# Attention scores of two maps in one tile of three PSUM banks, and a third bank for transposes and value products

## The chip, the cores and the metric

The kernel runs on one core of a Trainium2 chip. The metric is device time in microseconds (us) of one execution, as the median of several. TensorE (PE) multiplies matrices; its weight loads are shown as an engine of their own (PEld). VectorE (DVE) and ScalarE (ACT) read its results out of PSUM, which has eight banks of 512 float32 values for each of 128 partitions. Each engine takes its instructions in the order of its queue.

## What is computed

One inference step of a network of two layers, on 512 latent tokens and 128 prompt tokens, handled as one tile of 640 columns. The change lies in the first (even) layer, whose mixer has two kinds of attention heads. Four heads of kind A are differential: two attention maps on the same values, the second subtracted with a weight. Four pairs of heads of kind B are grouped-query attention, two heads of a pair on two halves of the partitions. In both, a block of 128 queries has two maps of scores, each softmaxed by itself:

```python
# kind A: two maps on the same values
a1 = block_attend(qa[:, :, None, :, :DH_A], k_a[..., :DH_A], v_a)[:, :, 0]
a2 = block_attend(qa[:, :, None, :, DH_A:], k_a[..., DH_A:], v_a)[:, :, 0]
oa = rms_norm(a1 - lam * a2, P['a_subln_g'][i]) * (1.0 - lam_init)
# kind B
ob = block_attend(qg, k_b, v_b)
# block_attend, for a block of 128 queries
sc = jnp.einsum('bgrqd,bgtd->bgrqt', qi, k).astype(F32) * scale
p = jax.nn.softmax(sc, axis=-1).astype(v.dtype)
return jnp.einsum('bgrqt,bgte->bgrqe', p, v)
```

Latent queries (blocks 0 to 3) see 256 cached and 512 own keys, 768 in all; prompt queries (block 4) see their own 128. A head so has four wide blocks and one narrow one, and the eight heads (counting a pair as one) 32 and 8.

## The kernel before

`even` (from L660) does the even layer. After the first projections it opens its PSUM pools: "g" has two banks for the whole kernel, and here "m" gets two banks and "S" two tiles of two banks (L683). The eight heads run in the order a0, a1, b0, b1, a2, b2, a3, b3 (`EV_HEADS`, L45). Beside them runs a stream of other work, `filling` (L906): the projections of the heads to come (tile "g"), the modulation of later layers (weights `wa`), norms and scalings of finished heads, and the first five eighths of the output projection. `in_turn` deals out head and filling by the numbers of `EV_FILL` (L47). On top of that the framework orders each engine's queue by a timeline of its own, so the queue isn't the order of the code.

A block of a head goes like this. `scores` (L753) takes two tiles of "S", one for each map, and multiplies: each map in two halves of 384 keys, one to a bank, and each half in two matmuls, since queries and keys are split into a rounded part and a rest (index `e`). Then for each map DVE takes the negated maximum `nm` (L766) and ACT the exponential with its sum, into `pr` (L768; four buffers). `scores` of block i+1 is called before block i goes on. For kind A (`attn_a`, L786) DVE joins the two maps into one (L798). `turned` (L773) transposes the probabilities on PE, three tiles of 128 to a bank of "m", and DVE or ACT copies them out to `PT` (L781). The value product goes to another bank of "m", and ACT copies it to `o` (L804, L825). `scale` (L834) spreads a row of factors over the partitions through "m" too, and DVE multiplies with it (L836). Splits of queries into the two parts are L726 on ACT and L728 on DVE.

After the heads the last three eighths of the output projection are done for all eight column tiles (L931), with their results in "S": one tile holds the two halves of the 640 tokens, one bank each. The function `halves` (L311) hands out these tiles. The feed-forward part of the layer, the odd layer, and its feed-forward follow.

Of the kernel before, what the change touches and what calls it, by code (L numbers as in the profile page):

```python
# [10 lines left out]
F32 = mybir.dt.float32  # L11
F32R = mybir.dt.float32r
U32 = mybir.dt.uint32
AF = mybir.ActivationFunctionType
ALU = mybir.AluOpType
AX = mybir.AxisListType
# [3 lines left out]
P = 128  # L20
# [271 lines left out]
class Trunk:  # L292
# [18 lines left out]
    def halves(self, tag="g", n=T):  # L311

        hs = slice(0, HT), slice(HT, n)
        if tag == "S":
            ps = self.pt(tag, [P, 2, 512])
            return [(ps[:, i, :h.stop - h.start], h) for i, h in enumerate(hs)]
        return [(self.pt(tag, [P, 512])[:, :h.stop - h.start], h) for h in hs]
# [342 lines left out]
    def even(self):  # L660
        nc, A = self.nc, self.A
        aps = [A["wev"][i] for i in range(18)]
        ident = self.con("ident")
        with ExitStack() as es:
# [18 lines left out]
            self.open_psum(m=2, S=2)  # L683
# [69 lines left out]
            def scores(q, k, i):  # L753
                k0, nb, w = (0, 2, 384) if i < 4 else (768, 1, 128)
                S = [self.pt("S", [P, 2, 512])[:, :nb, :w] for _ in range(2)]
                ic = slice(i * P, (i + 1) * P)
                for b in range(nb):
                    kc = slice(k0 + b * w, k0 + (b + 1) * w)
                    for m in range(2):
                        for e in range(2):  # L760
                            self.mm(S[m][:, b, :], q[:, m, e, ic], k[:, m, kc], start=e == 0, stop=e == 1)
                nm = ep.tile([P, 2], F32, tag="nm", bufs=4, name="nm")
                st = ep.tile([P, 2], F32, tag="st", bufs=4, name="st")
                pr = []
                for m in range(2):
                    nc.vector.tensor_reduce(nm[:, m:m + 1], S[m], AX.XY, ALU.max, negate=True)  # L766
                    t = ep.tile([P, 768], F32, tag="pr", bufs=4, name="pr")
                    nc.scalar.activation(t[:, :nb * w].rearrange("p (b w) -> p b w", b=nb), S[m], AF.Exp,  # L768
                                         bias=nm[:, m:m + 1], accum_out=st[:, m:m + 1])
                    pr.append(t[:, :nb * w])  # L770
                return pr, st, nb * w // P
# [159 lines left out]
        for m in range(KD):  # L931
            self.resid(m, self.gemm(A["wevo"][m, :, 5:], self.ohi[5:], self.olo[5:], "S"), self.modulation(0, 2))
# [794 lines left out]
```

## Time and profile before

| | us |
|---|---|
| median of three runs | 2186.5 |
| lowest, highest | 2181.66, 2186.52 |
| the profiled execution | 2182.15 |
| its span, first to last instruction | 2180.4 |
| PE busy in the span | 2080.5 (95%) |
| PEld, DVE, ACT busy | 1895.1, 1349.3, 1018.6 |
| mean granted clock of TensorE | 0.970 |
| even layer's heads, from the first scores to the closing product | 77 to 434 |
| closing product | 434 to 462 |
| odd layer | 1055 to 1640 |

The profile is of one execution, and times in it count from its first instruction. A row of the timeline gives start, duration, engine, line, operation, what is written and read, and in brackets how long the engine was idle before and what released it. Matmuls are pipelined: four matmuls in one row last less than four times a single one. A granted clock of 1.00 is full speed, 0.5 half of it.

### The profile page before, as it was taken

The page shows a single profiled execution, that of the slowest core. Times are in us where ns is not written, and L with a number is a line of the kernel's source. Part 1 is how long each engine was busy: PE and PEld are TensorE (multiplying, and loading weights), DVE is VectorE, ACT ScalarE, POOL GpSimd, SP SyncE. Part 2 cuts the span into 40 slices and gives each one's busy share as a digit, 9 for nine tenths or more (in the row PEclk, how much of TensorE's full clock was granted, in tenths as well). Part 3 has the DMA queues.
Part 4 walks back from the last instruction along what each step waited for, and adds up shares of the span by engine and source line. Part 5 has one row for each costly group of instructions (what it writes and reads, how often), then busy time and mean ns, then how long its engine had stood idle before and what let it go on. Part 6 is the DMA issues. An engine that isn't in the chain of part 4 may idle for free.

```text
span 2180.4 us, 44790 instructions
## 1 busy us (share of the span) xinstructions
PE 2080.5 (95%) x18461; PEld 1895.1 (87%) x18461; DVE 1349.3 (62%) x3067; ACT 1018.6 (47%) x2072; POOL 0.2 (0%) x4
## 2 busy tenths in 40 slices
PE   7899989999999999999999999898989999999997
PEld 5896778888899999989888788786777999999997
DVE  3858686557636647746774755745567674574663
ACT  4645464455414515546655545544344552452551
POOL 0000000000000000000000000000000000000000
PEclk9899999999999999999999999998989999999999
DMA  7114420125525222332542242332312222222212
GB/s 295 60 46 151 141 66 25 44 99 205 205 86 183 67 79 78 109 106 72 167 117 81 74 118 83 97 100 84 94 31 61 76 70 78 78 66 81 74 62 89
DMA packets 138061, 212.50 MB, mean 97 GB/s; under 512 B 51456, under 2 KB 68736, under 8 KB 131712
## 3 DMA queue, kind: packets, MB, share of 16 engines
q1 hardware_dynamic: 131168, 205.56, 29.2%
q10 hardware_dynamic: 6688, 4.07, 0.6%
q8 instruction: 145, 2.38, 0.5%
q14 instruction: 60, 0.49, 0.1%
HBM read 187.49 MB, written 22.09 MB: 96 GB/s over the span
## 4 chain that ended last, share of the span: by engine, by line
PE 85%; DVE 7%; DMA 4%; ACT 3%; issue 1%; SPq 0%; ACTq 0%; DVEq 0%
PE e L331 46%; PE g L331 21%; PE m L331 5%; PE pw L331 4%; PE S L331 3%; PE m L334 2%; DMA wa<-in_adaw 1%; PE gram L331 1%; PE pg L331 1%; PE HN L331 1%; PE O L331 1%; DMA in<-sp 1%; DVE wl L578 0%; ACT pr L768 0%; PE pg L334 0%
## 5 line engine op out<-in xcount | busy, mean ns | idle before, releaser
L331 PE MATMUL e<-hi,wh 128*128 128x320 f32 (+1 forms) x2240 | 693.4, 312 | 3.2 <-ACT hi L511 1.8
L331 PE MATMUL e<-lo,wh 128*128 128x320 f32 (+1 forms) x2240 | 695.5, 311 | 0.1
L331 PE MATMUL e<-hi,wl 128*128 128x320 f32 (+1 forms) x2240 | 691.3, 310 | 2.1 <-DVE wl L578 2.1
L577 ACT CAST wh<-wr 128x512 fp32r<-128x512 f32 (+3 forms) x434 | 237.6, 586 | 519.8 <-PE e L331 385.2
L331 PEld LDWEIGHTS e<-hi,wh 128*128 128x128 f32 x2240 | 421.4, 189 | 19.6 <-ACT tg L965 7.5
L331 PEld LDWEIGHTS e<-hi,wl 128*128 128x128 f32 x2240 | 422.9, 189 | 8.6 <-DVE wl L578 3.6
L331 PEld LDWEIGHTS e<-lo,wh 128*128 128x128 f32 x2240 | 422.5, 189 | 1.3 <-DVE lo L513 1.3
L578 DVE TENSOR_TENSOR wl<-wr,wh 128x512 fp32r<-128x512 f32 (+3 forms) x434 | 267.7, 647 | 74.5 <-ACT wh L577 73.9
L331 PE MATMUL g<-hi,wh 128*128 128x320 f32 (+1 forms) x928 | 302.9, 327 | 3.9 <-DVE x L625 1.3
L331 PE MATMUL g<-lo,wh 128*128 128x320 f32 (+1 forms) x928 | 296.0, 319 | 1.3 <-DVE lo L475 1.3
L331 PE MATMUL g<-hi,wl 128*128 128x320 f32 (+1 forms) x928 | 296.2, 319 | 0.0
L331 PEld LDWEIGHTS g<-hi,wh 128*128 128x128 f32 x928 | 178.4, 193 | 14.2 <-issue 2.2
L331 PEld LDWEIGHTS g<-lo,wh 128*128 128x128 f32 x928 | 178.3, 192 | 5.4 <-DVE lo L475 1.8
L331 PEld LDWEIGHTS g<-hi,wl 128*128 128x128 f32 x928 | 178.3, 192 | 2.5 <-issue 1.0
L625 DVE SCALAR_TENSOR_TENSOR x<-e,mod,x 128x320 f32<-128x320 f32 x168 | 67.0, 437 | 139.6 <-PE e L331 139.4
L966 ACT ACTIVATE tu<-tu,bias 128x512 f32<-128x512 f32 (+1 forms) x176 | 88.6, 548 | 0.0
L553 DVE TENSOR_SCALAR bias<-e 128x2 f32<-128x2 f32 x95 | 15.2, 159 | 117.1 <-PE e L331 117.1
L768 ACT ACTIVATE pr<-S,nm 128x768 f32<-128x768 f32 (+1 forms) x80 | 63.7, 797 | 47.5 <-DVE nm L766 28.1
L766 DVE TENSOR_REDUCE nm<-S 128x1 f32<-128x768 f32 (+1 forms) x80 | 65.1, 820 | 17.5 <-PE S L331 16.9
L976 ACT ACTIVATE tg<-tg 128x640 f32<-128x640 f32 x44 | 32.5, 739 | 79.9 <-DVE tg L943 79.9
L554 DVE TENSOR_TENSOR tu<-e,rstd 128x320 f32<-128x320 f32 x86 | 41.8, 488 | 38.3 <-PE e L331 38.2
L331 PE MATMUL g<-wa,csT 128*32 128x512 f32 x352 | 49.5, 635 | 12.1 <-DMA wa<-in_adaw 12.0
(398 smaller groups left out, 2914.5 us busy)
## 6 DMA issues: line engine op xcount, KB each, us to landing
wa<-in_adaw SPq DMA_DIRECT2D x48, 1024.0 KB
wr<-in_wup SPq DMA_DIRECT2D x176, 256.0 KB
wr<-in_wod SPq DMA_DIRECT2D x70, 256.0 KB
wr<-in_wdn SPq DMA_DIRECT2D x64, 256.0 KB
in<-sp SPq DMA_DIRECT2D x42, 320.0 KB
wr<-in_wev SPq DMA_DIRECT2D x36, 256.0 KB
wr<-in_wdn SPq DMA_DIRECT2D x32, 192.0 KB
x<-in_xT SPq DMA_DIRECT2D x8, 320.0 KB
```

Of the source, the lines that this page charges most:

```text
L331: self.nc.tensor.matmul(out, lhsT, rhs, start=start, stop=stop)
L334: self.nc.tensor.transpose(out, in_, ident)
L553: nc.vector.tensor_scalar(bias, p1[:, HT:], scale, None, op0=ALU.mult)
L554: nc.vector.tensor_tensor(t[:, :HT], p0, self.rs[:, :HT], op=ALU.mult)
L577: nc.scalar.copy(wh[:, a:b, :], wr)
L578: nc.vector.tensor_tensor(wl[:, a:b, :], wr, wh[:, a:b, :].bitcast(F32), op=ALU.subtract)
L625: nc.vector.scalar_tensor_tensor(o, ps, gate[:, m, s:s + 1], o, op0=ALU.mult, op1=ALU.add)
L766: nc.vector.tensor_reduce(nm[:, m:m + 1], S[m], AX.XY, ALU.max, negate=True)
L768: nc.scalar.activation(t[:, :nb * w].rearrange("p (b w) -> p b w", b=nb), S[m], AF.Exp, bias=nm[:, m:m + 1], accum_out=st[:, m:m + 1])
L966: nc.scalar.activation(u[:, a:b], u[:, a:b], AF.Identity, bias=b0[:, s:s + 1])
L976: nc.scalar.activation(gt, gt, AF.Silu)
```

## The change

The pools of this stretch become "m" with three banks and "S" with one tile, `Sb`, of three banks (1,536 values). Map 1 lies in its columns 0 to 767, map 2 in 768 to 1535, so the second bank holds the last 256 keys of map 1 and the first 256 of map 2. A map is multiplied in a piece of 512 and one of 256 keys, so that none crosses a bank. `Sb` is taken once and stays the same tile for all blocks. The maximum and the exponential read 768 columns in one row in place of 2 x 384. The closing product takes its two banks from "g" and "m" in turn, and `halves` loses its case for "S".

```diff
--- before.py
+++ after.py
@@ -311,9 +311,6 @@
     def halves(self, tag="g", n=T):
 
         hs = slice(0, HT), slice(HT, n)
-        if tag == "S":
-            ps = self.pt(tag, [P, 2, 512])
-            return [(ps[:, i, :h.stop - h.start], h) for i, h in enumerate(hs)]
         return [(self.pt(tag, [P, 512])[:, :h.stop - h.start], h) for h in hs]
 
     def in_halves(self, t):
@@ -680,7 +677,8 @@
             o = [ep.tile([P, T], F32, tag=f"o{j}", name=f"o{j}") for j in range(8)]
             head = [self.done(out, t, sc) for out, t, sc in zip(head, o[5:], (1.0, 0.125, 1.0))]
             self.pes.close()
-            self.open_psum(m=2, S=2)
+            self.open_psum(m=3, S=1)
+            Sb = self.pt("S", [P, 2, 768])
             rope = ep.tile([P, 2, NS], F32, name="rope")
             nc.scalar.dma_start(rope, A["rope"])
             shuf = [i ^ 16 for i in range(32)]
@@ -751,24 +749,23 @@
                 return vt
 
             def scores(q, k, i):
-                k0, nb, w = (0, 2, 384) if i < 4 else (768, 1, 128)
-                S = [self.pt("S", [P, 2, 512])[:, :nb, :w] for _ in range(2)]
+                k0, w = (0, 768) if i < 4 else (768, P)
                 ic = slice(i * P, (i + 1) * P)
-                for b in range(nb):
-                    kc = slice(k0 + b * w, k0 + (b + 1) * w)
-                    for m in range(2):
-                        for e in range(2):
-                            self.mm(S[m][:, b, :], q[:, m, e, ic], k[:, m, kc], start=e == 0, stop=e == 1)
+                for m in range(2):
+                    for a, b in ((0, 512), (512, 768)) if m == 0 else ((0, 256), (256, 768)):
+                        b = min(b, w)
+                        if a < b:
+                            for e in range(2):
+                                self.mm(Sb[:, m, a:b], q[:, m, e, ic], k[:, m, k0 + a:k0 + b], start=e == 0, stop=e == 1)
                 nm = ep.tile([P, 2], F32, tag="nm", bufs=4, name="nm")
                 st = ep.tile([P, 2], F32, tag="st", bufs=4, name="st")
                 pr = []
                 for m in range(2):
-                    nc.vector.tensor_reduce(nm[:, m:m + 1], S[m], AX.XY, ALU.max, negate=True)
-                    t = ep.tile([P, 768], F32, tag="pr", bufs=4, name="pr")
-                    nc.scalar.activation(t[:, :nb * w].rearrange("p (b w) -> p b w", b=nb), S[m], AF.Exp,
-                                         bias=nm[:, m:m + 1], accum_out=st[:, m:m + 1])
-                    pr.append(t[:, :nb * w])
-                return pr, st, nb * w // P
+                    nc.vector.tensor_reduce(nm[:, m:m + 1], Sb[:, m, :w], AX.X, ALU.max, negate=True)
+                    t = ep.tile([P, 768], F32, tag="pr", bufs=4, name="pr")[:, :w]
+                    nc.scalar.activation(t, Sb[:, m, :w], AF.Exp, bias=nm[:, m:m + 1], accum_out=st[:, m:m + 1])
+                    pr.append(t)
+                return pr, st, w // P
 
             def turned(pt, n, flip):
                 PT = ep.tile([P, 6, P], F32, tag="PT", bufs=2, name="PT")
@@ -929,7 +926,7 @@
                 self.dump(f"o{j}", o[j])
             self.warm_sqrt(o[EV_ORDER[7]][:, T - 1:])
         for m in range(KD):
-            self.resid(m, self.gemm(A["wevo"][m, :, 5:], self.ohi[5:], self.olo[5:], "S"), self.modulation(0, 2))
+            self.resid(m, self.gemm(A["wevo"][m, :, 5:], self.ohi[5:], self.olo[5:], "gm"[m % 2]), self.modulation(0, 2))
         self.pes.close()
         self.open_main_psum()
```

The instructions of PE change place. In the first head (a0) a block of queries has its scores `S<-kx,q`, and the rows `g<-hi` and `g<-lo` are one of the projections of `filling`. PE's queue before, from the head's first scores on:

```order
L331 MATMUL g<-hi_199,wl 128x322
L331 MATMUL S<-kx,q 128x384 x20
L331 MATMUL g<-hi_192,wh 128x320
L331 MATMUL g<-lo_200,wh 128x320
L331 MATMUL g<-hi_192,wl 128x320
L331 MATMUL g<-hi_193,wh 128x320
```

PE's queue after; the first block's eight matmuls and thirteen more rows of the same projection stand ahead of these:

```order
L328 MATMUL g<-lo_204,wh 128x320
L328 MATMUL g<-hi_196,wl 128x320
L328 MATMUL g<-hi_197,wh 128x320
L328 MATMUL g<-lo_205,wh 128x320
L328 MATMUL g<-hi_197,wl 128x320
L328 MATMUL g<-hi_198,wh 128x320
L328 MATMUL S<-kx,q 128x512 x2
L328 MATMUL S<-kx,q 128x256 x4
L328 MATMUL S<-kx,q 128x512 x2
L331 MATMUL m<-conT,pr 128x128 x6
```

Before, the matmuls of the first two blocks and a half of the third stood together, with the projection behind them. Now 19 matmuls of the projection stand between the first block and the second.

In the last head (b3), DVE's queue with the waits of each row; `nm<-S` are the maxima of the two maps of a block, `PT<-m` copies of transposed probabilities. The names in brackets say on which engine's counter the row waits. Before:

```order
L766 TENSOR_REDUCE nm<-S 128x1 [waits PE_49]
L818 RECIPROCAL rb<-st 128x2 [waits Activation_49]
L781 COPY PT<-m 128x384 [waits DVE_49,PE_49]
L766 TENSOR_REDUCE nm<-S 128x1 [waits PE_49]
L781 COPY PT<-m 128x384 [waits PE_49]
```

After:

```order
L764 TENSOR_REDUCE nm<-S 128x1 [waits PE_49]
L778 COPY PT<-m 128x384 [waits DVE_49,PE_49]
L764 TENSOR_REDUCE nm<-S 128x1 [waits Activation_49]
L778 COPY PT<-m 128x384 [waits DVE_49,PE_49]
L815 RECIPROCAL rb<-st 128x2 [waits Activation_49]
```

Before, both maxima wait for PE. Now the second one of a block waits for ACT, whose exponential of the first map stands on that counter.

In the same head, PE's queue; `m<-conT,pr` are transposes, `m<-PT,vtb` value products. Before:

```order
L331 MATMUL S<-kbx,q 128x384 x4
L334 MATMUL m<-conT,pr 128x128 x9
L331 MATMUL S<-kbx,q 128x384 x4
L331 MATMUL m<-PT,vtb 64x128 x12
L334 MATMUL m<-conT,pr 128x128 x3
L331 MATMUL S<-kbx,q 128x384 x4
L334 MATMUL m<-conT,pr 128x128 x9
L331 MATMUL S<-kbx,q 128x128 x2
```

After:

```order
L328 MATMUL S<-kbx,q 128x512 x2
L328 MATMUL S<-kbx,q 128x256 x4
L328 MATMUL S<-kbx,q 128x512 x2
L331 MATMUL m<-conT,pr 128x128 x6
L328 MATMUL m<-PT,vtb 64x128 x12
L331 MATMUL m<-conT,pr 128x128 x6
L328 MATMUL S<-kbx,q 128x512 x2
L328 MATMUL S<-kbx,q 128x256 x4
L328 MATMUL S<-kbx,q 128x512 x2
```

Before, the two maps' scores stood apart, with transposes or value products between. Now a block's eight matmuls stand together, and one block's second transposes, its value product and the next block's first transposes stand between two groups.

## Rows read from the trace of the kernel before

**Rows 1.** the page, part 1: busy us (share of span) xinstructions, by engine.
```profile
PE 2080.5 (95%) x18461; PEld 1895.1 (87%) x18461; DVE 1349.3 (62%) x3067; ACT 1018.6 (47%) x2072; POOL 0.2 (0%) x4
```

**Rows 2.** stretches: us; busy us by engine; granted clock, DMA, GB/s.
```profile
71.00:112.00 41.00, 34.12 (x200) 31.97 (x199) 38.59 (x77) 26.30 (x53) 0.00 (x0) 0.83 0.15 45
...
192.00:228.00 36.00, 32.36 (x219) 22.91 (x218) 29.93 (x52) 21.23 (x44) 0.00 (x0) 0.95 0.43 146
...
273.00:312.00 39.00, 33.92 (x244) 26.70 (x243) 36.21 (x74) 22.75 (x51) 0.00 (x0) 0.96 0.27 90
312.00:352.00 40.00, 34.61 (x247) 29.74 (x246) 25.17 (x52) 23.00 (x49) 0.00 (x0) 0.87 0.01 3
...
391.00:434.00 43.00, 39.04 (x314) 32.84 (x312) 22.23 (x47) 20.42 (x51) 0.00 (x0) 1.00 0.07 18
...
1055.00:1640.00 585.00, 546.34 (x8032) 470.86 (x8031) 357.20 (x892) 278.51 (x619) 0.00 (x0) 0.93 0.32 90
```

**Rows 3.** waits of PE's weight loads, 71 to 433: us, times, longest.
```profile
PEld S L331 <- ACT pr L768: 14.3, 16, 2.2
...
PEld m L334 <- DVE o L836: 4.8, 6, 1.5
...
PEld m L334 <- ACT PT L781: 4.0, 8, 1.3
...
PEld m L334 <- DVE PT L781: 2.6, 6, 0.9
...
PEld m L334 <- ACT o L804: 1.6, 1, 1.6
...
PEld m L334 <- ACT o L825: 0.9, 1, 0.9
```

**Rows 4.** by line and shape, 71 to 434: busy us, mean ns | idle.
```profile
L766 DVE TENSOR_REDUCE nm<-S 128x1 f32<-128x768 f32 x64 | 60.7, 954 | 15.5 <-PE S L331 14.9
...
L768 ACT ACTIVATE pr<-S,nm 128x768 f32<-128x768 f32 x64 | 57.8, 904 | 41.1 <-DVE nm L766 28.1 <-PE m L334 8.7 <-DVE s L795 2.0
...
L781 DVE COPY PT<-m 128x384 f32<-128x384 f32 x48 | 26.6, 555 | 27.8 <-PE m L334 27.6
...
L728 DVE TENSOR_TENSOR q<-o,q 64x640 fp32r<-64x640 f32 x20 | 16.4, 818 | 0.9 <-ACT q L726 0.7
```

**Rows 5.** timeline, PE, 77 to 92 (head a0): start, us, what.
```profile
83.98 1.65 PE L331 MATMUL S<-kx,q 128*128 128x384 f32 x4 [1.29 <-ACT pr L768]
86.95 1.65 PE L331 MATMUL S<-kx,q 128*128 128x384 f32 x4 [1.32 <-ACT pr L768]
90.31 1.65 PE L331 MATMUL S<-kx,q 128*128 128x384 f32 x4 [1.72 <-ACT pr L768]
```

**Rows 6.** timeline, DVE, 312 to 320 (head b2): first maxima of three blocks.
```profile
312.89 0.95 DVE L766 TENSOR_REDUCE nm<-S 128x1 f32<-128x768 f32 x1
...
315.94 0.96 DVE L766 TENSOR_REDUCE nm<-S 128x1 f32<-128x768 f32 x1 [0.79 <-PE S L331]
...
319.22 0.96 DVE L766 TENSOR_REDUCE nm<-S 128x1 f32<-128x768 f32 x1 [0.63 <-PE S L331]
```

**Rows 7.** timeline, all engines, 405 to 420 (head b3, no filling work left).
```profile
406.14 0.96 DVE L766 TENSOR_REDUCE nm<-S 128x1 f32<-128x768 f32 x1 [0.96 <-PE S L331]
...
410.70 0.20 ACT L768 ACTIVATION_READ_ACCUMULATOR pr<-S,nm 128x1 f32 x1
...
410.95 0.97 PE L331 MATMUL S<-kbx,q 128*128 128x384 f32 x4 [0.35 <-ACT pr L768]
...
411.85 1.53 PE L331 MATMUL m<-PT,vtb 128*64 128x128 f32 x24
...
411.96 0.96 DVE L766 TENSOR_REDUCE nm<-S 128x1 f32<-128x768 f32 x1 [0.76 <-PE S L331]
...
414.41 0.82 PE L334 MATMUL m<-conT,pr 128*128 128x128 f32 x6
...
416.89 0.29 DVE L766 TENSOR_REDUCE nm<-S 128x1 f32<-128x128 f32 x1 [0.23 <-PE S L331]
```

## Prediction

> **What bounds the kernel now.** I read the page's first line, then the table of stretches, then the waits of the matmul engine inside the one stretch that the change touches, and last the timeline of two places in it. On the page PE is busy 95% of the span and DVE 62% [rows 1]; the reader should take from it that PE is the bound on average, and that only time in which PE waits can be won or lost. The change lies in the even layer, between 71 and 434 us. The table of stretches shows that this is the least filled part: in 71 to 112 PE is busy 34.12 of 41 us, in 192 to 228 it is 32.36 of 36, in 273 to 312 it is 33.92 of 39 with DVE at 36.21, in 312 to 352 it is 34.61 of 40, in 391 to 434 it is 39.04 of 43 [rows 2]. The granted clock also falls there (0.83 in 71 to 112, 0.87 in 312 to 352), which is half speed, 1.2 of 2.4 GHz, for a part of those stretches, and it falls where PE has waits.
>
> The waits say for what. PE's weight loads waited 14.3 us for an exponential (L768) to give up a score bank, and for the other readers of PSUM that hold a bank of "m" they waited 4.8 (DVE's scaling, L836), 4.0 and 2.6 (the copies of transposed probabilities, L781), 1.6 and 0.9 (the copies of value products) [rows 3]. So the change trades on two sums of equal size: **14.3 us on score banks and 13.9 us on "m" banks**, of 363 us.
>
> **The change, part by part.**
>
> *Score matmuls.* A wide block keeps eight matmuls and 3,072 columns: 8 x 384 before, 4 x 512 and 4 x 256 after. Four of 384 take 0.97 us [rows 7], and at the same cost a column the new eight take the same. If the 256 wide ones were held to the pace of something narrower, 128 of them at 0.03 us more would cost 3.5 us; if wider ones run better, a gain of 1. I take 0.
>
> *The order of waits on scores.* This is the large term. Both maps now lie in one tile of three banks, and the second bank holds the end of map 1 and the start of map 2. The order of instructions shows what follows: DVE's first maximum waits for the last of all eight matmuls, its second maximum waits for ACT's first exponential, and the next block's first matmul waits for ACT's second exponential. Before, the second maximum waited for PE alone, and the next block could start behind the first exponential. A wide block is now a chain with nothing beside itself: eight matmuls 1.7 us from first start to last end (0.97 and another 0.7), maximum 0.954, exponential 0.904 and its sum read out 0.1 later, maximum 0.954, exponential 0.904 and 0.1 [rows 4, 7], and about 0.2 for the hand-overs (0.05 from the read-out to the next matmul [rows 7]): 5.8 us. The two maps before could run at 3.05 and 3.28 us a block where nothing else held them [rows 6]. 2.6 us more for each of 32 wide blocks would be 83 us with no cover. What covers it is PE's other work: 40 blocks (32 wide, 8 of one tile) stand in the 363 us, 9 us each, well over 5.8. So I counted, in the new order, the matmul work that stands between the end of one score group and the start of the next, at the paces of the trace. A group's last matmul is issued at 1.4 us of the 5.8, so 4.4 must be covered. In 24 of the 32 wide blocks there is more than that, mostly 5 to 7.5 us. In the other eight 2.0 to 3.7 us stand there, and the shortfall sums to 11 us. That is the lower end. The upper end: at a few places DVE's queue holds other work between the two maxima (eight instructions, some 5.9 us by their widths, in the second block of head b0; four splits of queries of 0.82 us each [rows 4] in the last blocks of b0 and a2), and the chain is longer by it; with these the shortfall is 27 us. I take 19, as not all of that work comes late. Against the 14.3 of before this is **+5 us, from -3 to +13**.
>
> Two places show both signs. In the first head before, five groups of four stand in a row ahead of a whole projection, and PE, which takes its queue in order, stood for 1.29, 1.32 and 1.72 us on exponentials at the half clock with 24 ready matmuls behind [rows 5]. After, 19 matmuls of that projection stand between the first two groups, and these waits mostly go. In the last head there is no filling work: 12 transposes and 12 value products, which PE issues as 24 (six transposes in 0.82, the 24 in 1.53 [rows 7]) give about 3 us against 4.4, so each block there waits 1.4 us and a block takes 5.8 us, where before two took 5.82 and 4.93 (starts 406.14, 411.96, 416.89 [rows 7]).
>
> *The third "m" bank.* It removes waits of transposes on copies: 4.0, 2.6, 1.6 and 0.9, which is 9.1 us. It can't remove the 4.8 on DVE's scaling, where DVE itself is what is slow [rows 3]. At most 9 goes; at least 2, since a product still needs its own copy, 0.555 us behind its transposes [rows 4], and in the blocks where the score chain is late PE waits there in place of here. I take **-6 us**.
>
> *DVE held up.* In its queue the second maximum now stands through an exponential (0.904 and 0.1 [rows 4]) with either nothing or one 0.555 copy ahead of it in about 18 wide blocks; some 13 us of DVE's time are lost. Behind it wait the copies of transposed probabilities and the evictions of the projections, and for these PE. DVE is busy 36.21 of 39 us in 273 to 312, but 25.17 of 40 in 312 to 352 [rows 2], so little comes through: **+2 us, 0 to 8**.
>
> *The closing product* moves from "S" to "g" and "m" in turn: four banks before, five now, and two products in flight both times. I take 0, from -1 to +2, since "m" is still in use by the last head's scaling.
>
> *Elsewhere.* The order shows the other layers as before up to the odd layer, whose instructions are dealt out anew in places. PE is busy 546.34 of 585 us there [rows 2]; of the 39 us that are left an eighth either way, 5 us, is my bound. I take 0.
>
> **Sum:** +5 - 6 + 2 = +1 us. The profiled execution took 2182.15 us; the median of the three runs is 2186.5, 4.35 more, so the forecast is 2182.15 + 1 + 4.35 = 2187.5, say **2187 us: no change that can be measured** (a measurement of this kernel can tell about 0.3%, 6.6 us).
>
> The same place was weighed against a page. The shared bank makes DVE's and ACT's reads take turns in the order; no run here shows what would happen without it. The Trainium skill (PSUM — Partial Sum Buffer, "PSUM bank collisions raise a hardware error") asks for just that: guard PSUM by bank and not by address, reads against reads included. By it the second wait can't be left out as long as the bank is shared, and the sum stands.
>
> **The rivals.**
>
> *Slower: the score chain decides.* With one set of score banks PE can't write the next block while the last is read. It decides wherever less than 4.4 us of other PE work stands between two groups, or where DVE's and ACT's queues lengthen the chain beyond the 5 to 7.5 us that are there elsewhere. For it: the row of 14.3 us is already the largest wait on a bank, and DVE is the busier partner in 273 to 312. Against it: the new order spaces the groups. Price: +13 on scores, 3 instead of 6 won on "m", +6 through DVE: +16, so 2203 us. The Trainium skill has this as a rule (Perfetto Trace Analysis, "Matmuls": independent groups should rotate through different banks, so that the eviction of one overlaps the matmuls of the next); the 3.05 us blocks agree with it.
>
> *Faster: the third bank and the new spacing win.* All 9 us of waits on copies go, the shortfall on scores is the 11 of the order alone (-3), and DVE's lost time hides: -12, so 2175 us. For it: the waits of the first head show that the old order held ready work behind scores. Against it: the last head has no work to put there.
>
> *The third bank does nothing.* The probabilities have four buffers, two blocks, and copies take 0.555 us whatever the number of banks. Then "m" saves 2, scores cost what they cost: +5, 2191 us, inside the forecast's band.
>
> **How the numbers follow.** No change (with the last rival in it): 0.38. Slower by over 0.3%: 0.32, at 2203. Faster by over 0.3%: 0.30, at 2175. The spread of the terms (scores 8 either way, "m" 3.5, DVE 4, the odd layer 5, the rest 2) adds in squares to 11 us; the range for 8 in 10 reaches somewhat past both rivals' times, 2169 to 2206. The forecast's own band is 2180 to 2193.
>
> **What would show it.** Right, if in the profile after PE's waits on the exponential in 71 to 434 come to some 19 us, in the last head and in b0 above all, those of transposes on copies fall under 4, DVE shows a new wait of its second maxima on ACT's exponential, and the stretch keeps its 363 us within 6. The chain is wrong if two score groups follow each other in under 5.7 us. The forecast is wrong if PE's waits on scores stay under 11 us, or if projections begin to wait for DVE; or if the odd layer's 585 us move by more than 5, which would have nothing to do with banks.

## The result, and the profile after

The changed kernel takes 2205.66 us (median of four, 2203.95 to 2208.73) against 2184.14 for the kernel before beside it: a ratio of 1.011, 95% interval 1.0094 to 1.0126. It is slower by 21.5 us, where no change was forecast. The profiled execution spans 2204.5 us against 2180.4, so 24.1 us are to be found in the traces. The page of the kernel after, its first lines (busy us and share of the span for each engine):

```profile
span 2204.5 us, 44781 instructions
PE 2091.2 (95%) x18461; PEld 1905.3 (86%) x18461; DVE 1350.7 (61%) x3067; ACT 1021.1 (46%) x2072; POOL 0.2 (0%) x4
```

Against [rows 1], PE is busy 10.7 us longer for the same 18,461 matmuls, and idle 13.4 us longer. DVE and ACT do the same work in the same time.

To see where, take two marks that both kernels have: the first matmul of the odd layer's Gram products (`gram`, L1424 and on), and its last state product (`HN`). In the kernel before they are at 1060.1 and 1648.4 us, after at 1067.7 and 1672.7, and from there to the end it is 532.0 and 531.8. So **7.6 us are lost ahead of the first mark, 16.7 between the two, nothing behind**. The change lies wholly ahead of the first mark. These marks are read from one profiled execution of each kernel, and executions differ (see the last section).

The next rows are of the view by stretches, one row each for before and after: first the even layer's heads, from the first score matmul to the last value product, then the odd layer from mark to mark. Columns: window, length, then busy time and instructions of PE, PEld, DVE, ACT, POOL, then the granted clock, DMA share, GB/s.

```profile
77.50:431.70 354.20, 325.50 (x2321) 279.58 (x2319) 249.20 (x502) 180.50 (x398) 0.00 (x0) 0.95 0.22 73
1060.10:1648.40 588.30, 547.79 (x8054) 471.54 (x8050) 357.01 (x895) 278.11 (x619) 0.00 (x0) 0.93 0.31 89
```

```profile
78.60:438.20 359.60, 323.43 (x2322) 278.59 (x2321) 249.66 (x502) 183.24 (x399) 0.00 (x0) 0.93 0.22 72
1067.70:1672.70 605.00, 560.64 (x8075) 483.90 (x8074) 360.19 (x903) 279.18 (x621) 0.00 (x0) 0.92 0.30 86
```

In the even layer PE's idle time goes from 28.7 to 36.2 us (length less busy), at a lower mean clock (1.00 is 2.4 GHz, 0.5 is 1.2, and a mean in between is some time at each). In the odd layer idle time hardly moves (40.5 and 44.4), and PE is busy 12.9 us longer, at 0.92 in place of 0.93. A part of that is more work between the marks: 8,074 weight loads in place of 8,050, since 24 matmuls of the odd layer's closing product now stand ahead of the second mark. From the first mark to the end of the program the work is the same, 11,482 weight loads, before and then after:

```profile
1060.10:2180.40 1120.30, 1064.20 (x11486) 972.14 (x11482) 679.24 (x1609) 503.52 (x1041) 0.00 (x0) 0.96 0.27 82
```

```profile
1067.70:2204.50 1136.80, 1075.26 (x11483) 981.44 (x11482) 679.83 (x1609) 504.00 (x1041) 0.00 (x0) 0.95 0.27 80
```

So of 16.5 us more, 11.1 are busy time for the same matmuls and 5.4 are idle time. What changed there is the order of instructions: of DVE's 1,240 rows in this layer 386 stand elsewhere.

The waits of PE's weight loads in the heads of the changed kernel (line, what for, us in total, times, longest), which answer to [rows 3]:

```profile
PEld g L328 <- DVE pf L551: 11.1, 2, 8.3
PEld S L328 <- ACT pr L766: 10.9, 8, 3.7
PEld m L328 <- ACT PT L778: 9.6, 9, 2.5
...
PEld m L328 <- DVE PT L778: 2.1, 2, 1.7
...
PEld m L331 <- ACT PT L778: 1.1, 2, 0.8
...
PEld m L331 <- DVE o L833: 0.6, 1, 0.6
```

The value products' waits for copies in the heads of the kernel before (its L331 is L328 here):

```profile
PEld m L331 <- ACT PT L781: 2.1, 3, 1.0
...
PEld m L331 <- DVE PT L781: 0.8, 4, 0.3
```

The transposes (L331 here, L334 before) hardly wait for a bank any more, and the wait for DVE's scaling falls from 4.8 to 0.6 (0.8 more is now waited by products). But value products (L328) now wait 11.7 us for copies, where they waited 2.9, and projections wait 11.1 us for an eviction by DVE. The first head shows the longest of these waits in the timelines of PE and DVE (start, us, operation; in brackets the idle time before):

```profile
82.55 0.86 PE L328 MATMUL S<-kx,q 128*128 128x256 f32 x3 [1.60 <-DVE q L726]
91.24 0.64 PE L328 MATMUL g<-hi,wh 128*128 128x320 f32 x1 [7.83 <-DVE pf L551]
```

```profile
89.78 0.95 DVE L764 TENSOR_REDUCE nm<-S 128x1 f32<-128x768 f32 x1
...
90.71 0.48 DVE L551 TENSOR_TENSOR pf<-g,rstd 128x320 f32<-128x320 f32 x1
91.11 0.48 DVE L552 TENSOR_TENSOR pf<-g,rstd 128x320 f32<-128x320 f32 x1
```

The eviction stands behind the second maximum in DVE's queue. It is not late by that: the kernel before did the same eviction at 90.55 us, and DVE is as full in both kernels from 82 to 92 us, 9.81 of 10 (the eviction before, the stretch before, the stretch after):

```profile
90.55 0.47 DVE L554 TENSOR_TENSOR pf<-g,rstd 128x320 f32<-128x320 f32 x1
```

```profile
82.00:92.00 10.00, 5.67 (x16) 4.15 (x15) 9.81 (x19) 4.81 (x9) 0.00 (x0) 0.50 0.22 66
```

```profile
82.00:92.00 10.00, 1.61 (x6) 1.18 (x7) 9.81 (x18) 3.67 (x7) 0.00 (x0) 0.59 0.20 66
```

Before, the projection started at much the same time, behind five score groups of which three had waited [rows 5]. So the wait has a new name; what is lost is that in these 8 us before three more score groups were made, and after none.

### The profile page after: what moved, and what is told of

Same layout as the page of the kernel before. It is cut to its first block, busy times and chain, and to the rows that moved or that the text cites. A ratio compares the mean times of both kernels' runs of the same rounds, so it can differ in the third digit from the quotient of the medians.

```text
span 2204.5 us, 44781 instructions
## 1 busy us (share of the span) xinstructions
PE 2091.2 (95%) x18461; PEld 1905.3 (86%) x18461; DVE 1350.7 (61%) x3067; ACT 1021.1 (46%) x2072; POOL 0.2 (0%) x4
## 4 chain that ended last, share of the span: by engine, by line
PE 84%; DVE 7%; DMA 4%; ACT 3%; issue 1%; SPq 0%; ACTq 0%; DVEq 0%
PE e L328 45%; PE g L328 20%; PE m L328 5%; PE pw L328 4%; PE S L328 2%; PE m L331 2%; PE gram L328 2%; PE pg L328 1%; PE HN L328 1%; PE O L328 1%; DMA wa<-in_adaw 1%; DVE wl L575 1%; DMA in<-sp 1%; PE pg L331 0%; DVE x L622 0%
## 5 line engine op out<-in xcount | busy, mean ns | idle before, releaser
L328 PE MATMUL e<-hi,wh 128*128 128x320 f32 (+1 forms) x2240 | 694.4, 313 | 4.1 <-ACT hi L508 1.8
L328 PE MATMUL e<-lo,wh 128*128 128x320 f32 (+1 forms) x2240 | 696.0, 311 | 0.1
L328 PE MATMUL e<-hi,wl 128*128 128x320 f32 (+1 forms) x2240 | 692.5, 311 | 1.9 <-DVE wl L575 1.9
L328 PEld LDWEIGHTS e<-hi,wh 128*128 128x128 f32 x2240 | 421.9, 189 | 22.3 <-ACT tg L962 7.5
L328 PEld LDWEIGHTS e<-hi,wl 128*128 128x128 f32 x2240 | 423.6, 189 | 8.3 <-DVE wl L575 3.7
L328 PEld LDWEIGHTS e<-lo,wh 128*128 128x128 f32 x2240 | 423.0, 189 | 1.8 <-DVE lo L510 1.3
L328 PE MATMUL g<-hi,wh 128*128 128x320 f32 (+1 forms) x952 | 312.9, 330 | 14.6 <-DVE pf L551 7.8
L328 PE MATMUL g<-lo,wh 128*128 128x320 f32 (+1 forms) x952 | 307.0, 323 | 0.0
L328 PE MATMUL g<-hi,wl 128*128 128x320 f32 (+1 forms) x952 | 304.6, 321 | 0.0
L328 PEld LDWEIGHTS g<-hi,wh 128*128 128x128 f32 x952 | 184.7, 194 | 27.4 <-DVE pf L551 8.3
L328 PEld LDWEIGHTS g<-hi,wl 128*128 128x128 f32 x952 | 184.8, 194 | 4.4 <-issue 1.7
L328 PEld LDWEIGHTS g<-lo,wh 128*128 128x128 f32 x952 | 185.3, 195 | 3.5 <-issue 0.8
L550 DVE TENSOR_SCALAR bias<-e 128x2 f32<-128x2 f32 x95 | 15.1, 159 | 114.6 <-PE e L328 114.6
L328 PE MATMUL g<-wa,csT 128*32 128x512 f32 x352 | 49.7, 650 | 14.2 <-DMA wa<-in_adaw 9.8
```

The lines of the kernel that those rows point to most:

```text
L328: self.nc.tensor.matmul(out, lhsT, rhs, start=start, stop=stop)
L550: nc.vector.tensor_scalar(bias, p1[:, HT:], scale, None, op0=ALU.mult)
```

## The experiments

All experiments are told in the terms of two things: the **score tiles** ("own": each map a tile of two banks, as before; "one": both maps in one tile) and the **order of the odd layer**, which the framework deals out anew when anything ahead of it moves. Three orders came up again and again: A, that of the kernel before; B, that of the changed kernel; C, a third. The framework also makes a new order in the even layer's heads whenever the score tiles or the banks change, so an experiment on these always has both in it.

### First round: parts of the change alone

```diff
 gm: the kernel before, and
-  ... self.olo[5:], "S"), ...
+  ... self.olo[5:], "gm"[m % 2]), ...
 a_cmg: the changed kernel, and
-  ... "gm"[m % 2]), ...
+  ... "mg"[m % 2]), ...
 after_m2_b: the changed kernel, and
-  self.open_psum(m=3, S=1)
+  self.open_psum(m=2, S=1)
+  self.tc.strict_bb_all_engine_barrier()    (ahead of self.odd())
 split_b: after_m2_b, and
-  Sb = self.pt("S", [P, 2, 768])
+  Sb = self.pt("S", [P, 2, 1024])           (both maps in pieces (0, 512), (512, 768))
```

> The kernel before with one edit alone: the closing product goes to "g" and "m" in turn in place of "S"; scores and their banks as before. By the order of instructions the even layer stays as it was but for some 180 matmuls around the closing product, while the odd layer is dealt out anew, within 15 DVE and 56 PE instructions as in the changed kernel. Theory 1 (two causes: the even layer's score chain costs some 8 us, and the new order of the odd layer another 16, with no bank involved): 2184 + 16 = 2200 us, the odd layer's stretch 16 us longer and the even layer's equal within 2. Theory 2 (the whole loss of 21 us comes from the new score banks, in the odd layer by what they shift, and the order there is worth nothing): 2184 us within 3.

> The changed kernel with one edit: the closing product takes "m" first and then "g", in place of "g" first. The scores and the three "m" banks are the changed kernel's; by the order of instructions the odd layer comes out nearly as in the kernel before (93 of 1240 DVE instructions elsewhere, in place of 386). Theory 1: the even layer's loss of 7.6 us stays and the odd layer's 16 us go: 2184 + 8 = 2192 us, range 2189 to 2196. Theory 2: 2206 us, as the changed kernel.

> The changed kernel with two "m" banks in place of three (the eighth bank is not used), and a barrier of all engines between the first feed-forward layer and the odd layer, which keeps the odd layer's order the same as in the next kernel. Against the even layer of the changed kernel (start of the feed-forward at 464.5 us in the profile, 7.6 us behind the kernel before at the odd layer) the third bank's worth shows: if it removes the waits of transposes on copies as forecast (6 us), the even layer ends some 6 us later than the changed kernel's; if it does nothing, within 2 us of it. The total has the barrier in it, some us.

> As the kernel with two "m" banks and the barrier, but the one score tile has four banks and each map lies in its own two, with pieces of 512 and 256 columns: no bank is shared by the two maps, and there is still one set of score banks. Theory A (the shared bank is what costs: the second maximum stands behind the first exponential): the second maxima wait no more for ACT, and the kernel is 8 us faster than the one with two "m" banks, range 4 to 15. Theory B (the one set of banks and the order of matmuls cost, not the sharing): within 3 us of it.

Measured: gm 2191.35 us (ratio 1.004, 1.0024 to 1.0056), a_cmg 2193.18 (1.0042, 1.003 to 1.0055), after_m2_b 2213.35, split_b 2208.8. a_cmg came where the theory of two causes put it, though by its trace the odd layer (594.6 us) gave back 10 of the 16. gm came between the two theories: its first Gram product is 2.1 us earlier than before's, and its odd layer takes 597.7 us, so the kernel loses 9.4 us in a layer that the edit doesn't touch, but not 16. after_m2_b gives two answers on the third bank. Its feed-forward starts at 464.2 us, as the changed kernel's (464.5), which the expectation reads as no effect; but against after_b of the second round, which differs by that bank alone, its first Gram product is 6.9 us later (1079.6 and 1072.7). split_b is 4.6 us faster than after_m2_b, inside the range of theory A, but not by A's cause: I had put the second maximum's wait down to the shared bank, and with unshared banks it stayed (18.1 us, against 16.9 with a shared one). Its first Gram product is even 1.8 us later than after_m2_b's, and the gain is in the odd layer (586.1 and 592.6 us). The framework's wait goes by the tile.

### Second round: the tile, and the order under a barrier

```diff
 split: split_b without the barrier
 pair: split, and
-  self.open_psum(m=2, S=1)
-  Sb = self.pt("S", [P, 2, 1024])
+  self.open_psum(m=2, S=2)
+  Sb = [self.pt("S", [P, 1024]) for _ in range(2)]     (in scores, for each block; Sb[m] for Sb[:, m])
 before_b, after_b: the kernels before and after, and
+  self.tc.strict_bb_all_engine_barrier()    (ahead of self.odd())
```

> The kernel with one score tile of four banks (each map in its own two, pieces of 512 and 256 columns, two "m" banks, closing product on "g" and "m"), without the barrier. The second maximum still stands behind the first exponential, since the wait goes by the tile. Its odd layer has the order of the kernel before (37 of 1240 DVE instructions elsewhere). If the one tile's chain costs the even layer's 8 us: 2184 + 8 = 2192 us. If the odd layer's loss came from the score banks after all: 2200 or more.

> As the one before it in this list, but each map's scores are a tile of their own (two tiles of two banks, as in the kernel before): the second maximum waits for PE alone, and the next block's first map can start behind the first exponential. Widths and order of the matmuls are the changed kernel's. Theory A (the chain through one tile is what costs in the even layer): the even layer is back at the time of before, 8 us faster than with one tile: 2184 us, range 2180 to 2188. Theory B (order and widths of the matmuls, or the closing product, cost): within 3 us of the one-tile kernel, 2192.

> The kernel before with a barrier of all engines ahead of the odd layer and nothing else. The even layer's order is untouched; the odd layer's order comes out as in the changed kernel (73 of 1240 DVE instructions elsewhere). If that order costs 9 to 16 us by itself, the stretch from the first Gram product to the last state product takes 597 to 605 us, where it took 588.3 before; if not, 588 within 4. The barrier itself adds some 10 us ahead of it, as in the two kernels that had it.

> The changed kernel with the same barrier. Its odd layer has nearly the order of the kernel before with the barrier (27 of 1240 DVE instructions and 69 of some 6000 matmuls elsewhere), so the two differ by the even layer. Theory 1: 8 us slower than that kernel, range 4 to 12. Theory 2 (the whole loss belongs to the score banks): 21 us slower.

Measured: split 2197.28 us, pair 2189.36, before_b 2206.45, after_b 2215.72. split is 5 us over its forecast, and pair, 1.4 us above the range of theory A, lies by its time within B's; the odd layers differ too, so only the stretches tell. split and pair have the same matmuls at the same widths in the same number of banks; they differ by one tile against two, and by the order that the framework makes of that: about half of PE's matmuls and of DVE's rows in the heads stand elsewhere. The first Gram product starts at 1070.0 in split and 1059.2 in pair. The rows of DVE's waits in the heads (all of its maxima, `nm`) of split, and then of pair:

```profile
DVE nm L764 <- PE S L328: 40.3, 29, 3.7
DVE nm L764 <- ACT pr L766: 17.3, 19, 1.9
```

```profile
DVE nm L764 <- PE S L328: 15.1, 24, 2.0
```

With a tile for each map the wait on the exponential is gone, that on scores falls to 15.1 us (16.9 in the kernel before), and the even layer is back at the time of before. **One tile in place of two costs the even layer 10.8 us** between these two. How much of it is the chain and how much the new order of the heads, this pair doesn't separate. But the 18 traces agree: from the first scores to the last value product the heads take 351.6 to 355.2 us with own tiles, in four different orders, 357.3 to 361.6 with one tile and three "m" banks, and 361.2 to 365.7 with one tile and two. The pair kernel is still 0.29% over the kernel before (0.15 to 0.42), all of it in the odd layer: 597.9 us in place of 588.3. The kernel before with nothing but a barrier, and with it an odd layer near order B, takes 601.6 us there. The barrier itself costs some 10 to 14 us from the first matmul of the feed-forward to the first Gram product (614.0 in split_b and 603.9 in split; 616.9 in gm_b and 603.1 in gm). after_b is 9.3 us slower than before_b, with almost equal odd orders: near the 8 expected, far from 21. That goes by medians; its trace is of an execution of 2203.87 us, where the other four took 2215 to 2217, and there the first Gram product is only 1.3 us behind that of before_b.

### Third round: is a like order enough?

```diff
 gm_b: gm, and
+  self.tc.strict_bb_all_engine_barrier()    (ahead of self.odd())
 mmaj: the kernel before, and
-  for b in range(nb):
-      kc = ...
-      for m in range(2):
+  for m in range(2):
+      for b in range(nb):
+          kc = ...
 after_m2: the changed kernel, and
-  self.open_psum(m=3, S=1)
+  self.open_psum(m=2, S=1)
```

> The kernel before with the barrier ahead of the odd layer and the closing product on "g" and "m". Against the kernel before with the barrier alone (2206 us) the even layer keeps its scores, and the odd layer comes out nearly in the order of the kernel before: 84 matmuls of its closing product stand behind the last state product, as there, in place of 60. If the order of the odd layer is what costs: 2206 - 13 = 2193 us, range 2189 to 2198, with 588 us within 5 from the first Gram product to the last state product. If the barrier and not the order made that kernel slow: 2204 to 2207.

> The kernel before with one edit: the score matmuls of map 1 all come ahead of those of map 2 (two tiles of two banks, 384 wide, as before). The first maximum can start behind four matmuls in place of six. If the even layer's time hangs on the order of the score matmuls, it ends some 3 us sooner or later than before's 431.7; if it hangs on the tiles alone, within 2 us of it. Its odd layer has an order between the others, with 60 matmuls of the closing product behind the last state product: 2184 + 5 to 13 us by that. A gain is possible only if the even layer gives more than that.

> The changed kernel once more, unedited, for a second profile and a time beside the others of this chip: 2206 us within 4. If its stretch from the first Gram product to the last state product is again 605 us within 4, that length belongs to the order; if it falls to 598 or less, as in its twin with the barrier, a part of the loss there is one execution's.

> The changed kernel with two "m" banks in place of three and nothing else: the direct price of the third bank in the even layer, read where the odd layer's first Gram product starts (1060.1 us in the kernel before, 1067.7 and 1067.5 in the two profiles of the changed kernel). Forecast's value, 6 us: 1073.6. What the one-tile kernel with two "m" banks and unshared score banks points to, 2 to 3 us: 1070. Third bank without effect: 1067.6 within 1.5. The odd layer has yet another order, so the total tells less: 2190 to 2212 us.

Measured: gm_b 2205.42 us, mmaj 2188.82 (1.002, 1.0005 to 1.0035), after_again 2197.98 (1.007, 1.0047 to 1.0092), after_m2 2181.2 (0.9993, 0.9983 to 1.0003). gm_b is a plain miss: 12 us over the forecast, its odd layer at 602.3 although only some 50 of DVE's 895 rows between the marks stand elsewhere than in order A. I had held that the 24 matmuls of the closing product which stand ahead of the last state product in some orders were the cause (8,074 weight loads between the marks in place of 8,050, as the rows show). That falls: gm_b has 8,050 and is slow, and after_m2 has 8,074 and is fast. Whether an order that is nearly alike is like enough, gm_b can't tell: its trace is of the slowest of six executions (2211.47 us), and the fastest, 2193.41, came where the forecast was. split, with 41 such rows, has an odd layer of 587.9 us, and split_b, with 7 and the barrier, 586.1.

after_again, the changed kernel unedited, missed its forecast too: its median, 2197.98, is 8 us under the 2206 within 4. Its trace, of an execution of 2207.04 us, has the odd layer at 606.7 us again. mmaj came at the lower end of its 2189 to 2197 us, with the heads ending at 431.4 as before and the odd layer at 596.9: the order of the score matmuls is worth nothing that shows there, the tiles being the same.

after_m2 was the surprise. It is the changed kernel without its third "m" bank, has the slower even layer that was expected (first Gram product at 1071.9, so the third bank is worth 4.2 us there), and yet is 24.5 us faster than the changed kernel in its first comparison (16.8 than in after_again) and as fast as the kernel before. Its odd layer has order C.

### Fourth round: equal orders, crossed

Small edits far from the odd layer were now chosen so that its order is, row by row on PE, DVE, ACT and SP, that of another measured kernel (in mmaj_sg but for one matmul).

```diff
 fill23: the kernel before, and
-EV_FILL = 17, 24, 11, 8, 7, 11, 16, 16
+EV_FILL = 17, 23, 11, 8, 7, 11, 16, 16
 mmaj_sg: mmaj, and
-  ... self.olo[5:], "S"), ...
+  ... self.olo[5:], "Sg"[m % 2]), ...
 mmaj_mg: mmaj, and "mg"[m % 2] there
 am2_mg: after_m2, and "mg"[m % 2] there
```

> The kernel before with 23 in place of 24 steps of filling work beside the second head; banks, score matmuls and closing product as before. Its odd layer has the order of the changed kernel, instruction by instruction on all engines. If that order alone costs: even layer within 3 us of before, odd layer (from the first Gram product to the last state product) 605 us within 8 as in the changed kernel, time 2184 + 13 = 2197 us, range 2191 to 2203. If the loss needs the changed banks: 588 and 2184.

> The kernel before with the score matmuls of map 1 ahead of those of map 2 and the closing product on "S" and "g" in turn. Its odd layer has the order of the changed kernel with two "m" banks (one matmul apart), which ran 574.8 us from the first Gram product to the last state product. If the order alone decides, the even layer stays within 2 us of before's and the odd layer gains 13.6: 2184 - 14 = 2170 us, range 2165 to 2177, faster than both kernels. If the gain there came from the one-tile even layer ahead of it: 2184 or more.

> As the one before it, but the closing product goes to "m" and "g" in turn, and the odd layer has the order of the kernel before, instruction by instruction. If the order decides: 588 us within 5 in the odd layer and 2183 us within 4, where the same score matmuls with another odd order took 2188.8.

> The changed kernel with two "m" banks, closing product on "m" first and then "g": one tile of three banks for the scores, and the odd layer of the kernel before, instruction by instruction. If the odd layer goes by its order and the even layer by its chain: 588 us within 5 in the odd layer, the first Gram product 10 to 12 us later than before's, 2184 + 11 = 2195 us, range 2191 to 2199; against it the same kernel with the other closing order took 2181.2.

All four times came within their ranges, mmaj_sg at the fast end of its own. Of the stretches, am2_mg's odd layer is 1.6 us over its band and its first Gram product 0.7 (its trace is of the slowest of six executions, 2201.15 us), and fill23's first Gram product is 3.7 us behind that of before. With the kernels before, after and after_m2 they fill a table of two kinds of even layer and three orders of the odd one:

| kernel | scores, "m" banks | odd order | us | ratio to before | first Gram | odd layer |
|---|---|---|---|---|---|---|
| before | own, 2 | A | 2183.0 | 1 | 1060.1 | 588.3 |
| mmaj_mg | own, 2 | A | 2179.84 | 0.9988 (0.9979 to 0.9998) | 1058.2 | 589.0 |
| am2_mg | one, 2 | A | 2193.65 | 1.0051 (1.0036 to 1.0066) | 1072.8 | 594.6 |
| fill23 | own, 2 | B | 2197.6 | 1.0068 (1.0055 to 1.0081) | 1063.8 | 602.8 |
| after | one, 3 | B | 2205.66 | 1.011 (1.0094 to 1.0126) | 1067.7 | 605.0 |
| after_again | one, 3 | B | 2197.98 | 1.007 (1.0047 to 1.0092) | 1067.5 | 606.7 |
| mmaj_sg | own, 2 | C | 2165.09 | 0.9921 (0.9909 to 0.9933) | 1061.6 | 574.4 |
| after_m2 | one, 2 | C | 2181.2 | 0.9993 (0.9983 to 1.0003) | 1071.9 | 574.8 |

The times are of different comparisons, each with its own runs of the kernel before, so the ratios are what to compare; the last two columns are of one execution each. They tell most of the story: the start of the odd layer goes by the score tiles (1058.2 to 1063.8 us with own tiles, 1067.5 to 1072.8 with one), and its length by its order (574 to 575 in C, 588 to 595 in A, 603 to 607 in B). Here are the rows of the odd layer from mark to mark of mmaj_mg (A), fill23 (B), after_m2 and mmaj_sg (both C), each from its own trace, columns as above:

```profile
1058.20:1647.20 589.00, 543.75 (x8057) 468.18 (x8051) 357.10 (x896) 277.90 (x619) 0.00 (x0) 0.94 0.31 89
```

```profile
1063.80:1666.60 602.80, 561.70 (x8075) 484.38 (x8074) 360.08 (x903) 279.28 (x621) 0.00 (x0) 0.92 0.31 87
```

```profile
1071.90:1646.70 574.80, 541.20 (x8074) 468.46 (x8074) 359.20 (x903) 279.31 (x621) 0.00 (x0) 0.95 0.32 91
```

```profile
1061.60:1636.00 574.40, 542.96 (x8084) 470.31 (x8074) 357.83 (x904) 279.33 (x621) 0.00 (x0) 0.94 0.32 91
```

The reader should compare PE's busy time and the clock. Order B makes PE busy for 561 to 564 us at 0.92, A for 544 to 550 at 0.93 to 0.94, C for 541 to 543 at 0.94 to 0.95, and in C it is idle for 31 to 34 us where it is 40 to 45 in A and B. Which score tiles stand ahead makes little difference to that, 0.4 us in C and 2 to 4 in B: fill23 never had a shared tile and shows the changed kernel's odd layer. In A it is 6, in am2_mg's trace of 2201.15 us.

**mmaj_sg beats both kernels**: 2165.09 us, 0.8% under the kernel before. But its gain is that of an order which came by chance; the edit itself (score matmuls by maps) is worth nothing measurable in the even layer, whose last value product ends at 431.7 us as before.

## Why the prediction was wrong

Taken by the steps of the sum.

**Elsewhere (0, bound 5 either way): this step failed, and decided the sign.** It measured +16.7 us. The prediction saw that the odd layer is dealt out anew, and bounded what that may cost by an eighth of PE's 39 idle us. That counted waits alone. The new order costs mostly by PE's busy time, at a lower clock: 11.1 us for the same matmuls from the first mark to the end, against 5.4 of idle time. In fill23, with the tiles and banks of before and order B, the same stretch has 10.7 us more of busy time and 1.2 of idle time than before:

```profile
1063.80:2196.00 1132.20, 1074.89 (x11483) 981.39 (x11482) 679.51 (x1609) 504.08 (x1041) 0.00 (x0) 0.95 0.27 81
```

A bound from measured rows would have to be about three times wider: the orders met here run from 574 to 607 us in this layer. The prediction's last paragraph named this as what would make it wrong and said that it would have nothing to do with banks. The crossed runs show that: with the score banks of before, order B makes the odd layer 14.5 us longer (fill23, whose trace has 3.7 us lost ahead of it too and 2.5 won behind; its median is 14.6 us over that of before), and order C makes the kernel 14.8 us faster (mmaj_sg against mmaj_mg).

**The score chain and DVE held up (+5 and +2): right mechanism, price too low.** One tile with two "m" banks starts the odd layer at 1070.0, 1071.9 and 1072.8 us, two tiles with the same widths at 1059.2: 11 to 14 us, where 7 were forecast, the new order of the heads included. The chain's length was right: 5.8 us was worked out for a block, the first maxima of neighbouring wide blocks never start less than 5.77 us apart in the changed kernel, and in the last head they stand 6.40, 5.93 and 5.77 us apart. The new wait of the second maxima on ACT is there as well (12.0 us). Two blocks of the last head show both, and the last row is the sum over all heads:

```profile
419.91 0.96 DVE L764 TENSOR_REDUCE nm<-S 128x1 f32<-128x768 f32 x1 [1.57 <-PE S L328]
...
421.93 0.96 DVE L764 TENSOR_REDUCE nm<-S 128x1 f32<-128x768 f32 x1 [0.59 <-ACT pr L766]
...
425.68 0.96 DVE L764 TENSOR_REDUCE nm<-S 128x1 f32<-128x768 f32 x1 [1.57 <-PE S L328]
```

```profile
DVE nm L764 <- ACT pr L766: 12.0, 15, 1.6
```

What was wrong is where the price shows. The forecast looked for 19 us of waits on the exponential, and these are 10.9; under 11, and projections waiting for DVE (11.1 us), were its own signs of being wrong. The delay comes out at other places: at value products whose probabilities come late, and at a projection that stands ahead of the next scores and waits for an eviction. The prediction had read that place in the first head as ready matmuls held up behind scores, which the new spacing would set free. They were hardly ready: the eviction that they wait for after, at 90.71 us, came no earlier than 90.55 before.

**The third "m" bank (-6): right sign and about the right size.** One tile with three banks starts the odd layer at 1067.7, 1067.5 and 1066.4, so the bank is worth some 4.4 us; in the three pairs of kernels that differ by it alone it is 4.2, 6.3 and 6.9, each with a new order of the heads. Waits of transposes fell below 4 as forecast. That it couldn't touch the wait for DVE's scaling was wrong, as these rows of after_m2 (two banks) show beside the 0.6 of the changed kernel:

```profile
PEld m L328 <- ACT PT L778: 6.7, 11, 1.8
PEld m L331 <- DVE o L833: 6.4, 6, 2.2
...
PEld m L331 <- ACT PT L778: 4.0, 3, 3.1
PEld m L331 <- DVE PT L778: 2.1, 4, 0.7
```

Some of what the bank removes comes back: value products wait 11.7 us for copies with three banks and 8.4 with two.

**Widths and the closing product (0).** pair, which has both, starts the odd layer 0.9 us ahead of before, and gm, which has the closing product alone, 2.1 us: 1.1 beyond the stated band. (The upper price of the narrow matmuls, 128 at 0.03 us, is 3.8 us and not 3.5; nothing hangs on it.)

So the even layer lost 7.6 us where the sum said 1. That alone would have been at the edge of what a measurement shows. Of the rivals, the slower one had the right time (2203) with the wrong main cause, which is luck; the third bank was not without effect.

As to the pages cited: that independent groups should rotate through banks, so that evictions overlap matmuls (the Trainium skill, Perfetto Trace Analysis, "Matmuls"), agrees with these traces, in that the kernels without that overlap have the longer heads. split against pair does not price the number of banks, which is the same in both; the 10.8 us are what one tile cost, the new order of the heads included. The rule on guarding PSUM by bank (the Trainium skill, PSUM — Partial Sum Buffer, "PSUM bank collisions raise a hardware error") was not what made the second maximum wait. It waits 16.9 us with a shared bank (after_m2) and 17.3 with unshared ones (split), with almost the same order in the heads and the same length of these (361.6 and 362.1 us), because the framework tracks the tile.

**What stays open.** Why order B costs and C gains is shown only as PE's busy time, idle time and clock, not traced to one instruction. How far the lower clock is a cause or itself a mark of the order, no run here separates. From the first mark to the end, the clock records of the traces have PE at the lower level for 95 us in the kernel before, 110 in the changed one and 109 in fill23. Four score matmuls take 1.65 us there [rows 5] and 0.97 at full clock [rows 7]; by these, 15 us more would make some 6 of the 11 us, an estimate, and the rest is not told. In the even layer the chain and the new order of the heads are not separated. And the 21.5 us of the first comparison were 14.2 in the second, so the shares of 7.6 and 16.7 us are those of profiled executions.

## What to carry to other kernels

Where a framework orders the queues, an edit also deals out the work behind it anew. Compare the order of instructions far from the edit first, and where it moved, put a price on it from the spread of orders that were measured, not from the waits that are there. To judge the edit itself, look for a harmless second edit that brings the old order back, row by row, and compare those two. And two readers of one PSUM tile took turns here even where their banks were different, and the kernels with such a tile had the longer heads: give each its own tile.

## What the runs showed of the hardware

Two executions of one kernel differ by up to 18 us, and the granted clock goes with it: the changed kernel took 2192.2 us at a mean of 0.966 and 2207.4 at 0.961, and gm_b 2193.4 at 0.970 and 2211.5 at 0.964. The kernel before lay within 2177.5 to 2191.5 in the 17 executions beside these.

The same matmuls, from the first Gram product to the end of the program, kept PE busy 1,075 to 1,078 us in order B, 1,060 to 1,067 in order A and 1,055 to 1,057 in order C, while its idle time was 57 to 62 us in B, 56 to 61 in A and 48 to 50 in C. I had looked for the price of an order in waits; between A and B nearly all of it is in busy time.
